# The y of a Hyena layer kept by thirds of the tokens in the storage of the projections' input, with the last two projections in a written order

## The chip, the cores and the metric

The kernel runs on one core of a Trainium2 chip. The metric is the device time of one execution in microseconds (us). The engines are TensorE (PE for matmuls, PEld for the weight loads that overlap them), VectorE (DVE), ScalarE (ACT), GpSimd (POOL) and SyncE (SP), which issues most of the DMAs. Each engine works its own instructions in the order in which they stand; semaphores order the engines against each other.

## The reference

Two layers over 1024 latent tokens (tiles 0 to 7 of 128) and 128 context tokens (tile 8), with width 1024. The part that matters here is the end of layer 0 (Hyena) and the start of layer 1 (attention):

```python
proj = h @ w_in                                   # 1024 -> 4096, 32 groups of 128 columns
u = short_conv(proj[..., :3 * HY_WIDTH], conv_w, conv_b)
gate = proj[..., 3 * HY_WIDTH:]
x0, x1, v = jnp.split(u, 3, axis=-1)
...                                               # y = long convolution of z = v * x1
y = (y + z * f_bias) * x0
out = (y * jax.nn.silu(gate)) @ w_out
x = x + g * out
h1 = rmsnorm(x, norm_w[1]) * (1.0 + scale) + shift
proj1 = h1 @ mla_w_in                             # the first projection of layer 1
```

## The kernel before, in words

Everything is float32. A product is made of three matmul passes: each operand is split into a high part (float32r, made on ACT or POOL by `hi`, L88 and L90) and the rest (`lo`, a subtraction on DVE or POOL, L96); high by high, high by rest and rest by high are summed in PSUM.

The input of layer 0, transposed (channels on the partitions), lies as three thirds of 384 tokens: `hT0` to `hT2` (high) and `lT0` to `lT2` (rest), each 128 x 8 x 384. A projection `in_proj` takes one of the 32 column groups of w_in: for each third 3 x 8 matmuls of 128x384. Its weights come in two halves (`wi_raw`, 256 KB each, issued on SP): ACT makes `wi_h` of a half and POOL `wi_l`. The convolved projections go through `conv_cb` (a copy into `u`) and `conv` (one instruction on ACT, two on DVE over all 1152 tokens).

The inverse transforms write y of each of the eight channel groups to HBM (`YD`) and later read it back (`y0` to `y7`, 576 KB each). Groups 6 and 7 are gated last, by `gate_group`: projection g, convolution, projection 24 + g, SiLU, product. For group 7 these are projections 7 and 31, the last two of all.

When projection 31 is done, the pool of the input (`hy`) is released, and `lhh0` to `lhh7`, `lhl0` to `lhl7` (one 128x1152 tile per channel group) take its place: eight `hi` on ACT and eight `lo` on DVE. `w_out` then multiplies tile by tile of the tokens, 24 matmuls of 128x512 per tile and half of the columns, adds to x, and `norm_mod` writes the input of layer 1 back over `lhh` and `lhl`, in pairs of tiles: a square and a root on ACT, a scaling `nm_x` on DVE, eight transposes per tile on PE, `nm_h` on ACT, high part on POOL, rest on DVE. The list `WT` groups the tiles: 0-3, 4-5, 6-7, 8. While the last tiles are normed, PE works on `mla_gate(0)` (L970), 144 matmuls of 128x384, of which 96 need only the first two thirds of the tokens.

The order of each engine's instructions is not that of the source: a scheduler sets it from a modelled timeline, with priorities (`urgent`) and lower bounds (`issue_after`). Within `manual_schedule` the named engines keep the written order; the others don't.

Of the kernel before, what the change touches and what calls it, by code (L numbers as in the profile page):

```python
# [17 lines left out]
P = 128  # L18
# [2 lines left out]
GATES = (0, None, None, 1, None, None, None, None)  # L21
NY = 6
YP, YG = (), ()
WT = ((0, 1, 2, 3), (4, 5), (6, 7), (8,))
XB = 4
PLAN = "g2 I0 a0 I1 g3 I2 a1 I3 g4 a2 g5 I4 a3 i5 i6 i7"
WRB = 3
# [48 lines left out]
class K:  # L76
# [107 lines left out]
    def norm_mod(self, xs, tiles, pool, ps, A, B, hT, lT):  # L184

        N = P * len(tiles)
        ys = [pool.tile([P, D], F32, name="nm_x", tag="nm_x", bufs=2) for _ in xs]
        self.norm(xs, ys, pool)
        c = 1 if tiles[0] == 8 else 0
        o = slice(P * tiles[0], P * tiles[0] + N)  # L190
        for k in range(8):
            pt = self.turn(ys, k, ps, "nm_ps", 3)
            h = pool.tile([P, 256], F32, name="nm_h", tag="nm_h", bufs=3)
            self.S.activation(h[:, :N], pt, AF.Identity, bias=B[:, k, c:c + 1], scale=A[:, k, c:c + 1])
            self.hi("pool", hT[k][:, o], h[:, :N])
            self.lo("dve", lT[k][:, o], h[:, :N], hT[k][:, o])
# [458 lines left out]
    def hyena(self):  # L655
# [141 lines left out]
        with self.urgent():  # L797
            for g in range(8):
                if g in late and g not in done:
                    self.gate_y(g, ys[g], q, yb)  # L800
        for g in range(8):
            if g not in GATES and g not in late:
                with tc.issue_after(last):
                    self.gate_group(g, q, ys[g])
        early.release()
        hy.release()
        lh = tc.alloc_tile_pool(name="lh", bufs=1, side="left", reuse_waits="tile")
        lhh, lhl = [], []
        for g in range(8):
            lhh.append(lh.tile([P, T], F32R, name=f"lhh{g}"))  # L810
            lhl.append(lh.tile([P, T], F32R, name=f"lhl{g}"))
            self.hi("pool" if g in HP else "act", lhh[g], ys[g])
            self.lo("pool" if g in YP else "dve", lhl[g], ys[g], lhh[g])
        yb.release()
        ips.release()
        A = self.small.tile([P, 8, 2], F32, name="ada_A1")
        self.ada_mod(1, m1, A, slice(0, 8))
        return lh, lhh, lhl, wp, wo, gd, (A, m1[:, 0:8, :])

    def w_out(self, px, wp, ps, lhh, lhl, wo, gd, A, B):  # L820

        nc, a = self.nc, self.a
        wo.append(self.load_w(a["w_out"][1], px, 512, "wo1", 1, raw_bufs=WRB, step=1))
        gb = self.load_gate(px, gd, "gb0")
        for tiles in WT:
            xs = [self.load_x(px, t, XB) for t in tiles]
            for h in range(2):
                o = slice(512 * h, 512 * h + 512)
                for x, t in zip(xs, tiles):
                    pt = ps.tile([P, 512], F32, name="wo_ps", tag="wo_ps", bufs=4)  # L830
                    self.mm3(pt, lhh, lhl, slice(P * t, P * t + P), *wo[h], 8)
                    tm = px.tile([P, 512], F32, name="wo_t", tag="wo_t", bufs=1)
                    self.tt(tm, pt, gb[:, 1 if t == 8 else 0, o], ALU.mult)
                    self.tt(x[:, o], x[:, o], tm, ALU.add, self.G)
            for x, t in zip(xs, tiles):
                nc.sync.dma_start(self.x1d[t], x)
            for i in range(0, len(tiles), 2):
                self.norm_mod(xs[i:i + 2], tiles[i:i + 2], px, ps, A, B, lhh, lhl)
# [74 lines left out]
    def mla_in(self, pool, wpool, ps, hT, lT, m):  # L913
        nc, a = self.nc, self.a
        qnh, qnl, ckh, ckl, kp = m["qnh"], m["qnl"], m["ckh"], m["ckl"], m["kp"]
        qkv = pool.tile([P, NT, 672], F32, name="qkv", bufs=1)
        for h in range(2):
            wh, wl = self.load_w(a["wm_a"][h], wpool, 336, "wm", 2, raw_bufs=2, step=1, tag_raw="wm_raw")
            for t in range(NT):
                pt = ps.tile([P, 512], F32, name="wo_ps", tag="wo_ps", bufs=4)  # L920
                self.mm3(pt[:, :336], hT, lT, slice(P * t, P * t + P), wh, wl, 8)
                self.S.copy(qkv[:, t, 336 * h:336 * h + 336], pt[:, :336])
        kvr = pool.tile([P, KVL], F32, name="kvr", bufs=1)
        nc.sync.dma_start(kvr, a["kv_norm"].partition_broadcast(P))
        rt = pool.tile([P, 2, 8, ROPE], F32, name="rope_k", bufs=1)
        nc.sync.dma_start(rt, a["rope_k"])
        rq, ck = [], []
        for t in range(NT):
            r = self.rstd(pool, qkv[:, t, 0:QL], QL, "q")
            self.V.tensor_scalar(qkv[:, t, 0:QL], qkv[:, t, 0:QL], r, None, ALU.mult)  # L930
            r = self.rstd(pool, qkv[:, t, QL:QL + KVL], KVL, "kv")
            kv = qkv[:, t, QL:QL + KVL]
            self.stt(kv, kv, r, kvr, ALU.mult)
        nc.sync.dma_start(a["s_ckv"], qkv[:, 8, QL:QL + KVL])
        nc.sync.dma_start(a["s_kpe"], qkv[:, 8, QL + KVL:672])
        for g in range(3):
# [24 lines left out]
    def mla_gate(self, h, pool, ps, hT, lT, GD, bufs):
        wh, wl = self.load_w(self.a["wm_g"][h], pool, 256, "wm", bufs, raw_bufs=2, step=1, tag_raw="wm_raw",
                             size=336 if h else 256)
        for o in range(0, T, 384):
            for i in range(2):
                w = slice(P * i, P * i + P)
                pt = ps.tile([P, 512], F32, name="wo_ps", tag="wo_ps", bufs=4)[:, :384]
                for k in range(8):
                    for s, (a, b) in enumerate(((wh, hT), (wl, hT), (wh, lT))):
                        self.PE.matmul(pt, a[:, k, w], b[k][:, o:o + 384], start=s == 0 and k == 0, stop=s == 2 and k == 7)  # L970
                g = pool.tile([P, 384], F32, name="gsil", bufs=GB)
                self.S.activation(g, pt, AF.Silu)
                (self.nc.sync if h else self.nc.scalar).dma_start(GD[2 * h + i][:, o:o + 384], g)
# [544 lines left out]
```

## Time and profile before

| | |
|---|---|
| time, median of 3 runs | 1785.12 us (1783.82 to 1785.66) |
| profiled execution | 1784.39 us |
| its span in the trace | 1782.2 us |
| busy: PE, PEld, DVE, ACT, POOL | 97%, 87%, 70%, 61%, 31% |
| chain that ended last | PE 75%, DVE 13%, DMA 4%, ACT 3%, issue 3% |
| mean granted TensorE clock | 0.997 |

The profiled execution is 2.2 us longer than its span, and 0.7 us below the median of the runs. PE is busy nearly throughout, so what a change in this stretch is worth is read from the few places at which PE has nothing to do, and from the clock that it is granted (1.00 is 2.4 GHz, 0.50 is 1.2 GHz). Times below are from the start of the span.

### The profile page before, as it was taken

The numbers are of one execution on the slowest core, as the hardware profiler recorded it, in microseconds if no ns is written. First come the engines' busy times: TensorE is split into PE (matmuls) and PEld (weight loads), VectorE is DVE, ScalarE is ACT, GpSimd is POOL, SyncE is SP. The second block draws the span as 40 slices with busy tenths as digits, with TensorE's granted clock in tenths as the row PEclk, the third lists the DMA queues.
The fourth block names the chain that finished last, engine by engine and source line by source line (L and its number), as shares of the span: only waits on it lengthen the run. The fifth ranks groups of instructions, "written<-read, shape, count | busy, mean of one in ns | idle before, by whom it ended". The sixth has DMA issues, their size and how long they took to land.

```text
span 1782.2 us, 29982 instructions
## 1 busy us (share of the span) xinstructions
PE 1728.2 (97%) x10704; PEld 1555.8 (87%) x10704; DVE 1245.5 (70%) x2515; ACT 1087.0 (61%) x2566; POOL 550.1 (31%) x771
## 2 busy tenths in 40 slices
PE   6999999999999999999999999999999999999998
PEld 4888889999999788888999889999999998999876
DVE  4658988999886895542242487878887888778464
ACT  7656557665654334324352587878887888788441
POOL 3335234343443101232000134433433343227300
PEclk9999999999999999999999999999999999999999
DMA  8233332111133856422213310100010010003351
GB/s 332 92 114 108 103 99 89 57 51 48 55 110 124 273 173 246 154 78 81 71 47 98 88 31 27 39 25 25 25 38 26 23 30 25 19 20 92 128 186 73
DMA packets 90488, 156.99 MB, mean 88 GB/s; under 512 B 11683, under 2 KB 57923, under 8 KB 88548
## 3 DMA queue, kind: packets, MB, share of 16 engines
q1 hardware_dynamic: 85744, 145.29, 24.8%
q0 software_dynamic: 2272, 6.38, 1.2%
q10 hardware_dynamic: 2324, 3.42, 0.6%
q8 instruction: 84, 1.38, 0.3%
q14 instruction: 64, 0.52, 0.1%
HBM read 113.92 MB, written 36.73 MB: 85 GB/s over the span
## 4 chain that ended last, share of the span: by engine, by line
PE 75%; DVE 13%; DMA 4%; ACT 3%; issue 3%; POOL 2%; SPq 0%; DVEq 0%; ACTq 0%; POOLq 0%
PE wo_ps L627 14%; PE wo_ps L1309 12%; PE ip_ps L426 10%; PE av_ps L1193 9%; PE nm_ps L1181 7%; PE wo_ps L970 5%; PE wo_ps L1005 5%; PE iv_ps L556 3%; PE df_ps L375 2%; DMA wi_raw<-w_in 2%; DVE pr_o L99 2%; DVE cv L102 1%; PE nm_ps L1037 1%; DVE O L102 1%; POOL wi_l L96 1%
## 5 line engine op out<-in xcount | busy, mean ns | idle before, releaser
L1309 PE MATMUL wo_ps<-kT,qT 128*128 128x512 f32 (+1 forms) x1152 | 278.7, 372 | 4.9 <-ACT prob L1316 4.4
L1316 ACT ACTIVATE prob<-wo_ps,mx 128x512 f32<-128x512 f32 (+1 forms) x384 | 234.1, 618 | 13.0 <-DVE mx L1314 11.1
L88 ACT ACTIVATE pt_h<-nm_ps 128x512 fp32r<-128x512 f32 x324 | 192.9, 599 | 74.0 <-PE nm_ps L1181 67.1
L1312 DVE TENSOR_REDUCE mx<-wo_ps 128x1 f32<-128x512 f32 (+1 forms) x384 | 213.0, 596 | 22.7 <-PE wo_ps L1309 22.1
L1309 PEld LDWEIGHTS wo_ps<-kT,qT 128*128 128x128 f32 x1152 | 187.4, 189 | 39.4 <-ACT prob L1316 14.4
L96 DVE TENSOR_TENSOR pt_l<-nm_ps,pt_h 128x512 fp32r<-128x512 f32 x324 | 210.5, 683 | 14.6 <-ACT pt_h L88 10.4
L96 POOL TENSOR_TENSOR wi_l<-wi_raw,wi_h 128x512 fp32r<-128x512 f32 x64 | 121.6, 1900 | 243.7 <-ACT wi_h L88 238.2
L1181 PE MATMUL nm_ps<-ident,prob 128*128 128x128 f32 x1280 | 191.4, 272 | 0.0
L426 PE MATMUL ip_ps<-hT,wi_h 128*128 128x384 f32 x720 | 153.0, 343 | 5.9 <-ACT wi_h L88 5.9
L1181 PEld LDWEIGHTS nm_ps<-ident,prob 128*128 128x128 f32 x1280 | 149.9, 140 | 8.5
L426 PE MATMUL ip_ps<-lT,wi_h 128*128 128x384 f32 x720 | 154.0, 342 | 0.0
L426 PE MATMUL ip_ps<-hT,wi_l 128*128 128x384 f32 x720 | 150.1, 342 | 0.0
L426 PEld LDWEIGHTS ip_ps<-hT,wi_h 128*128 128x128 f32 x720 | 126.1, 189 | 14.6 <-ACT wi_h L88 6.8
L1193 PE MATMUL av_ps<-pt_h,Vt 128*128 128x256 f32 x640 | 137.8, 297 | 0.0
L1193 PE MATMUL av_ps<-pt_l,Vt 128*128 128x256 f32 x640 | 135.0, 292 | 0.1
L426 PEld LDWEIGHTS ip_ps<-lT,wi_h 128*128 128x128 f32 x720 | 126.9, 189 | 5.2 <-issue 2.5
L426 PEld LDWEIGHTS ip_ps<-hT,wi_l 128*128 128x128 f32 x720 | 126.6, 189 | 5.5 <-issue 2.1
L99 POOL TENSOR_TENSOR pr<-ev 128x256 f32<-128x256 f32 x72 | 77.0, 1075 | 130.0 <-ACT ev L383 75.4
L1193 PEld LDWEIGHTS av_ps<-pt_l,Vt 128*128 128x128 f32 x640 | 97.6, 188 | 8.2 <-DVE pt_l L96 2.1
L1193 PEld LDWEIGHTS av_ps<-pt_h,Vt 128*128 128x128 f32 x640 | 97.9, 189 | 0.2
L102 DVE SCALAR_TENSOR_TENSOR cv<-u,cols,cv 128x1153 f32<-128x1153 f32 x48 | 75.7, 1578 | 11.8 <-ACT cv L451 11.7
L1200 POOL COPY rr<-sm 128x128 f32<-128x128 f32 x64 | 18.4, 288 | 202.4 <-DVE sm L1199 201.8
(355 smaller groups left out, 4083.1 us busy)
## 6 DMA issues: line engine op xcount, KB each, us to landing
wi_raw<-w_in SPq DMA_DIRECT2D x64, 256.0 KB, 3.0
ada_w<-ada_w SPq DMA_DIRECT2D x12, 1024.0 KB, 7.4
ada_w<-ada_w SPq DMA_DIRECT2D x24, 512.0 KB, 3.9
x_in<-xs SPq DMA_DIRECT2D x16, 512.0 KB, 5.2
PS<-pr_o SPq DMA_DIRECT2D x64, 128.0 KB, 1.9
pi_raw<-PS SPq DMA_DIRECT2D x32, 256.0 KB, 4.0
YD<-yv SPq DMA_DIRECT2D x8, 576.0 KB, 3.5
y<-YD SPq DMA_DIRECT2D x8, 576.0 KB, 9.1
```

The source lines that it names most:

```text
L88: self.S.activation(out, src, AF.Copy)
L96: e.tensor_tensor(out, src, hi.bitcast(F32), ALU.subtract)
L99: (eng or self.V).tensor_tensor(out, x, y, op)
L102: self.V.scalar_tensor_tensor(out, x, s, y, op0, op1)
L426: mm = self.PE.matmul(pt, w[:, k, :], x[c][:, k, :], start=s == 0 and k == 0, stop=s == 2 and k == 7)
L627: self.PE.matmul(pt, x[k][:, sl], w[:, k, :], start=s == 0 and k == 0, stop=s == 2 and k == kt - 1)
L970: self.PE.matmul(pt, a[:, k, w], b[k][:, o:o + 384], start=s == 0 and k == 0, stop=s == 2 and k == 7)
L1181: self.PE.transpose(pt[:, P * i:P * i + P], u["p"][i % 2][n // 2][:, P * (2 * (n % 2) + i // 2):P * (2 * (n % 2) + i // 2) + P], self.ident)
L1193: self.PE.matmul(u["po"][:, :256], m["V"][:, 2 * n + e, j, :], u[n][1 + s][:, 256 * e:256 * e + 256], start=n == first and e + s == 0, sto ...
L1309: self.PE.matmul(pt[:, :n], x[:, j, P * i:P * i + P], y[:, j, o:o + n], start=s == 0, stop=s == 2)
L1312: self.V.tensor_reduce(mx[:, b:b + 1], c["s", i, b][:, :n], AX.X, ALU.max)
L1316: self.S.activation(c["p"][i][b], c["s", i, b][:, :n], AF.Exp, bias=c["mx"][i][:, 3:4], accum_out=c["sm"][:, i, b:b + 1])
```

## The change

y is no longer split as a whole into sixteen tiles after the last projection. It is split by thirds of the tokens, and each third takes the tile of the input third that it replaces (`hT0`, `lT0` and so on, by their names), as soon as both last projections have read that third. A new `gate_last` does group 7: projections 7 and 31 run for the first two thirds, then for the last one; the order of ACT and DVE there is written out; the product with y and its split are made per third. `w_out` takes its tiles by three, three, two and one, and `norm_mod`, still in pairs, so norms tiles 2 and 5 alone. What reads the thirds later (`tokens`) is changed to match.

```diff
-WT = ((0, 1, 2, 3), (4, 5), (6, 7), (8,))
+WT = ((0, 1, 2), (3, 4, 5), (6, 7), (8,))
...
@@ norm_mod
-        o = slice(P * tiles[0], P * tiles[0] + N)
+        third, o = tiles[0] // 3, P * (tiles[0] % 3)
+        o = slice(o, o + N)
+        hT, lT = ([x[third][:, k] for k in range(8)] for x in (hT, lT))
...
@@ hyena
-        for g in range(8):
-            if g not in GATES and g not in late:
-                with tc.issue_after(last):
-                    self.gate_group(g, q, ys[g])
+        with tc.issue_after(last):
+            self.gate_group(6, q, ys[6])
+            lhh, lhl = self.gate_last(7, q, hy, ys)
         early.release()
-        hy.release()
-        lh = tc.alloc_tile_pool(name="lh", bufs=1, side="left", reuse_waits="tile")
-        lhh, lhl = [], []
-        for g in range(8):
-            lhh.append(lh.tile([P, T], F32R, name=f"lhh{g}"))
-            lhl.append(lh.tile([P, T], F32R, name=f"lhl{g}"))
-            self.hi("pool" if g in HP else "act", lhh[g], ys[g])
-            self.lo("pool" if g in YP else "dve", lhl[g], ys[g], lhh[g])
...
+    def gate_last(self, g, q, hy, ys):
...
+        def weights(i):
+            k = slice(4 * i, 4 * i + 4)
+            raw = pool.tile([P, 4, P], F32, name="wi_raw", bufs=1)
+            self.nc.sync.dma_start(raw, self.a["w_in"][24 + g][:, k])
+            self.hi("act", hs[0][:, k], raw)
+            self.lo("pool", hs[1][:, k], raw, hs[0][:, k])
+
+        def project(w, c):
+            pt = q["ips"].tile([P, 384], F32, name="ip_ps", tag="ip_ps", bufs=3)
+            for s, (a, x) in enumerate(((w[0], self.hT), (w[0], self.lT), (w[1], self.hT))):
+                for k in range(8):
+                    self.PE.matmul(pt, a[:, k, :], x[c][:, k, :], start=s == 0 and k == 0, stop=s == 2 and k == 7)
+            return pt
...
+        def product(c):
+            for o, o_, n in parts(c):
+                self.tt(gt[:, o:o + n], gt[:, o:o + n], x0[:, o:o + n], ALU.mult)
+                self.tt(y[:, o_:o_ + n], y[:, o_:o_ + n], gt[:, o:o + n], ALU.mult)
+
+        def split(c, gs):
+            if lhh[c] is None:
+                lhh[c], lhl[c] = (hy.tile([P, 8, 384], F32R, name=f"{x}T{c}") for x in "hl")
+            for i in gs:
+                x = ys[i][:, 384 * c:384 * c + 384]
+                self.hi("act", lhh[c][:, i], x)
+                self.lo("dve", lhl[c][:, i], x, lhh[c][:, i])
+
+        with self.tc.manual_schedule(engines={E.Activation, E.DVE}):
+            weights(0)
+            self.conv_cb(project(w0, 0), 0, q)
+            weights(1)
+            self.conv_cb(project(w0, 1), 384, q)
+            silu(project(hs, 0), 0)
+            split(0, range(7))
+            silu(project(hs, 1), 1)
+            self.conv_cb(project(w0, 2), 768, q)
+            x0 = self.conv(g, q)
+            split(1, range(7))
+            for c in range(2):
+                product(c)
+                split(c, (7,))
+            silu(project(hs, 2), 2)
+            product(2)
+            split(2, range(8))
```

Upstream of projection 7 no engine's order is changed; from there to the end of the last norm they are.

On PE, the last two projections before the change: `wi_h_7109` and `wi_l_7110` are the weights of projection 7, `wi_h_7202` and `wi_l_7203` those of projection 31; the number after `ip_ps` tells the third's accumulator, and x4 are the matmuls of one half of the weights.

```order
L426 MATMUL ip_ps_7213<-hT1_123,wi_l_7110 128x384 x8
L426 MATMUL ip_ps_7239<-hT2_125,wi_l_7110 128x384 x8
L426 MATMUL ip_ps_7239<-lT2_126,wi_h_7109 128x384 x8
L426 MATMUL ip_ps_7239<-hT2_125,wi_h_7109 128x384 x8
L426 MATMUL ip_ps_7271<-hT0_121,wi_h_7202 128x384 x4
L426 MATMUL ip_ps_7297<-hT1_123,wi_h_7202 128x384 x4
L426 MATMUL ip_ps_7323<-hT2_125,wi_l_7203 128x384 x4
L426 MATMUL ip_ps_7271<-hT0_121,wi_h_7202 128x384 x4
```

And with the change (projection 7 as before, projection 31 with `wi_h_7177` and `wi_l_7178`):

```order
L835 MATMUL ip_ps_7216<-hT1_123,wi_l_7110 128x384 x8
L835 MATMUL ip_ps_7242<-hT0_121,wi_h_7177 128x384 x4
L835 MATMUL ip_ps_7284<-hT1_123,wi_h_7177 128x384 x4
L835 MATMUL ip_ps_7242<-hT0_121,wi_h_7177 128x384 x4
L835 MATMUL ip_ps_7242<-lT0_122,wi_h_7177 128x384 x8
L835 MATMUL ip_ps_7242<-hT0_121,wi_l_7178 128x384 x4
L835 MATMUL ip_ps_7284<-hT1_123,wi_h_7177 128x384 x4
L835 MATMUL ip_ps_7284<-lT1_124,wi_h_7177 128x384 x2
L835 MATMUL ip_ps_7242<-hT0_121,wi_l_7178 128x384 x4
L835 MATMUL ip_ps_7284<-lT1_124,wi_h_7177 128x384 x6
L835 MATMUL ip_ps_7284<-hT1_123,wi_l_7178 128x384 x8
L835 MATMUL ip_ps_7310<-hT2_125,wi_h_7109 128x384 x8
```

Before, all of projection 7 and the first half of projection 31 for three thirds stand ahead of the first matmul that needs the second half of the weights. Now 28 matmuls fewer stand there: the last third of projection 7 (24) is behind it, and so are four of the last third of 31.

On SP, the loads around that second half (`wi_raw`), with `y5` to `y7` the read-back of y and `w_raw` weights of w_out. Before:

```order
L796 DMA y5_6942<-YD5_109 128x1152
L410 DMA wi_raw_7208<-w_in 128x512
L796 DMA y6_6943<-YD6_110 128x1152
L619 DMA w_raw_6975<-w_out 128x512
L796 DMA y7_6944<-YD7_111 128x1152
L619 DMA w_raw_7419<-w_out 128x512
L619 DMA w_raw_7423<-w_out 128x512
L619 DMA w_raw_7427<-w_out 128x512
```

With the change:

```order
L799 DMA y5_6942<-YD5_109 128x1152
L799 DMA y6_6943<-YD6_110 128x1152
L799 DMA y7_6944<-YD7_111 128x1152
L622 DMA w_raw_6975<-w_out 128x512
L827 DMA wi_raw_7212<-w_in 128x512
L622 DMA w_raw_7444<-w_out 128x512
L622 DMA w_raw_7448<-w_out 128x512
L622 DMA w_raw_7452<-w_out 128x512
```

The second half of the weights of projection 31 is now issued behind y6, y7 and a piece of w_out instead of ahead of them.

On PE, near the end of the norms: `nm_ps` x4 are the last transposes of tiles 6 and 7, x5 the first of tile 8, and the `wo_ps` rows between are the gate projection of layer 1. Before, 32 matmuls stand between the two, of which the first rows are:

```order
L181 MATMUL nm_ps<-ident,nm_x 128x128 x4
L970 MATMUL wo_ps<-lhh_7379,wm_l 128x384
L970 MATMUL wo_ps<-lhl_7380,wm_h 128x384
L970 MATMUL wo_ps<-lhh_7383,wm_h 128x384
L970 MATMUL wo_ps<-lhh_7383,wm_l 128x384
L970 MATMUL wo_ps<-lhl_7384,wm_h 128x384
```

With the change there are 6:

```order
L182 MATMUL nm_ps<-ident,nm_x 128x128 x4
L1035 MATMUL wo_ps<-hT_7341,wm_h 128x384
L1035 MATMUL wo_ps<-hT_7341,wm_l 128x384
L1035 MATMUL wo_ps<-lT_7342,wm_h 128x384
L1035 MATMUL wo_ps<-hT_7341,wm_h 128x384
L1035 MATMUL wo_ps<-hT_7341,wm_l 128x384
L1035 MATMUL wo_ps<-lT_7342,wm_h 128x384
L182 MATMUL nm_ps<-ident,nm_x 128x128 x5
```

The 26 others stand ahead of the x4 now; ACT's and DVE's instructions between the two are the same as before.

## Rows read from the trace of the kernel before

**Rows 1.** The page, busy time of PE with its share of the span and count.

```profile
PE 1728.2 (97%) x10704; PEld 1555.8 (87%) x10704; DVE 1245.5 (70%) x2515; ACT 1087.0 (61%) x2566; POOL 550.1 (31%) x771
```

**Rows 2.** Stretches: length, busy PE PEld DVE ACT POOL, granted clock, DMA share, GB/s.

```profile
685.80:690.70 4.90, 4.90 (x28) 4.45 (x26) 1.39 (x2) 2.70 (x5) 0.00 (x0) 1.00 1.02 402
690.70:692.80 2.10, 0.00 (x1) 0.00 (x0) 1.34 (x2) 0.97 (x2) 0.00 (x0) 1.00 1.04 406
692.80:694.25 1.45, 1.44 (x8) 1.44 (x9) 1.45 (x3) 0.01 (x1) 1.42 (x1) 1.00 1.04 406
694.25:697.65 3.40, 3.40 (x13) 3.40 (x12) 3.40 (x3) 0.63 (x1) 1.04 (x1) 0.52 1.06 410
697.65:705.10 7.45, 7.42 (x43) 7.10 (x41) 0.86 (x2) 0.99 (x2) 0.00 (x0) 0.99 0.15 60
705.10:706.76 1.66, 0.00 (x0) 0.00 (x0) 1.23 (x2) 1.65 (x4) 0.00 (x0) 1.00 0.00 0
706.76:755.80 49.04, 49.03 (x211) 39.52 (x212) 28.75 (x38) 18.98 (x29) 11.19 (x8) 1.00 0.41 138
```

**Rows 3.** The chain that ended last, in order of time: start, length, what.

```profile
692.81 12.28 PE ip_ps L426 x60
```

**Rows 4.** Timeline of SP's issues (start, length, line, out<-in, count).

```profile
680.86 1.75 SPq L796 DMA_DIRECT2D y<-YD  x2
683.79 0.33 SPq L410 DMA_DIRECT2D wi_raw<-w_in  x1
...
685.89 0.33 SPq L619 DMA_DIRECT2D w_raw<-w_out  x1
686.50 0.32 SPq L796 DMA_DIRECT2D y<-YD  x1
```

**Rows 5.** Timeline of DVE and ACT: first users of what SP loaded.

```profile
691.46 1.36 DVE L99 TENSOR_TENSOR y<-y,xg 128x1152 f32<-128x1152 f32 x1 [1.51 <-DMA y<-YD]
692.13 0.63 ACT L88 ACTIVATE wi_h<-wi_raw 128x512 fp32r<-128x512 f32 x1 [1.08 <-DMA wi_raw<-w_in]
694.25 0.63 ACT L88 ACTIVATE wo_h<-w_raw 128x512 fp32r<-128x512 f32 x1 [1.49 <-DMA w_raw<-w_out]
```

**Rows 6.** The page, DMA issues: count, KB each, median us to landing.

```profile
wi_raw<-w_in SPq DMA_DIRECT2D x64, 256.0 KB, 3.0
...
y<-YD SPq DMA_DIRECT2D x8, 576.0 KB, 9.1
```

**Rows 7.** Timelines of ACT and DVE: convolution, and instructions on a third's 384 columns.

```profile
647.44 0.56 DVE L99 TENSOR_TENSOR bf<-bf 128x384 f32<-128x384 f32 x1
...
689.14 0.36 ACT L443 COPY u<-ip_ps 128x256 f32<-128x256 f32 x1
...
689.69 1.35 ACT L451 ACTIVATE cv<-u,cols 128x1153 f32<-128x1153 f32 x1
...
696.50 1.41 DVE L102 SCALAR_TENSOR_TENSOR cv<-u,cols,cv 128x1153 f32<-128x1153 f32 x1
...
701.64 0.49 ACT L508 ACTIVATE cv<-ip_ps 128x384 f32<-128x384 f32 x1 [1.24 <-PE ip_ps L426]
```

**Rows 8.** Timelines of ACT and DVE: the split of y, then second-half weights of w_out.

```profile
705.55 8.54 ACT L88 ACTIVATE lhh<-y 128x1152 fp32r<-128x1152 f32 x8
...
718.36 1.89 DVE L96 TENSOR_TENSOR wo_l<-w_raw,wo_h 128x512 fp32r<-128x512 f32 x3
```

**Rows 9.** The chain near the end of the norms (as Rows 3).

```profile
825.53 0.44 PE nm_ps L181 x4
825.97 5.56 PE wo_ps L970 x32
```

**Rows 10.** Timelines of ACT, DVE and PE in the same stretch.

```profile
826.25 1.05 ACT L171 ACTIVATE nm_x<-x_in 128x1024 f32<-128x1024 f32 x1
...
828.24 1.28 ACT L172 ACT_TABLE_LOAD   x1
...
830.12 0.75 DVE L176 TENSOR_SCALAR nm_x<-x_in,nm_r 128x1024 f32<-128x1024 f32 x1
...
831.35 0.49 PE L181 MATMUL nm_ps<-ident,nm_x 128*128 128x128 f32 x3
...
832.44 0.68 PE L181 MATMUL nm_ps<-ident,nm_x 128*128 128x128 f32 x2 [0.60 <-ACT nm_h L194]
```

More of the change, by code (lines that the diff above doesn't have):

```diff
@@ L817, in hyena, with parts, silu @@
         self.ada_mod(1, m1, A, slice(0, 8))
-        return lh, lhh, lhl, wp, wo, gd, (A, m1[:, 0:8, :])
+        return hy, lhh, lhl, wp, wo, gd, (A, m1[:, 0:8, :])
+    def gate_last(self, g, q, hy, ys):
+        assert q["order"][q["n"]] == g and q["order"][q["n"] + 1] == 24 + g
+        pool, u, y = q["early"], q["u"], ys[g]
+        w0, w1 = q["w"], [[], []]
+        hs = [pool.tile([P, 8, P], F32R, name="wi_" + x, bufs=2) for x in "hl"]
+        gt = pool.tile([P, 1153], F32, name="cv", bufs=3)
+        lhh, lhl = [None] * 3, [None] * 3
+        def weights(i):
[10 more added lines that the diff above has]
+            return pt
+        def parts(c):
+            return ((384 * c, 384 * c, 384),) if c < 2 else ((768, 768, 256), (1025, 1024, P))
+        def silu(pt, c):
+            d = 0
+            for o, _, n in parts(c):
+                self.S.activation(gt[:, o:o + n], pt[:, d:d + n], AF.Silu)
+                d += n
+        def product(c):
[9 more added lines that the diff above has]
+                self.lo("dve", lhl[c][:, i], x, lhh[c][:, i])
+        E = mybir.EngineType
+        with self.tc.manual_schedule(engines={E.Activation, E.DVE}):
[15 more added lines that the diff above has]
+            split(2, range(8))
+        return lhh, lhl
@@ L820, in w_out, with tokens @@
+    def tokens(self, x, t):
+        return [x[t // 3][:, k, P * (t % 3):P * (t % 3) + P] for k in range(8)]
     def w_out(self, px, wp, ps, lhh, lhl, wo, gd, A, B):
@@ L830, in w_out @@
                     pt = ps.tile([P, 512], F32, name="wo_ps", tag="wo_ps", bufs=4)
-                    self.mm3(pt, lhh, lhl, slice(P * t, P * t + P), *wo[h], 8)
+                    self.mm3(pt, self.tokens(lhh, t), self.tokens(lhl, t), slice(0, P), *wo[h], 8)
                     tm = px.tile([P, 512], F32, name="wo_t", tag="wo_t", bufs=1)
@@ L920, in mla_in @@
                 pt = ps.tile([P, 512], F32, name="wo_ps", tag="wo_ps", bufs=4)
-                self.mm3(pt[:, :336], hT, lT, slice(P * t, P * t + P), wh, wl, 8)
+                self.mm3(pt[:, :336], self.tokens(hT, t), self.tokens(lT, t), slice(0, P), wh, wl, 8)
                 self.S.copy(qkv[:, t, 336 * h:336 * h + 336], pt[:, :336])
@@ L969, in mla_gate @@
                     for s, (a, b) in enumerate(((wh, hT), (wl, hT), (wh, lT))):
-                        self.PE.matmul(pt, a[:, k, w], b[k][:, o:o + 384], start=s == 0 and k == 0, stop=s == 2 and k == 7)
+                        self.PE.matmul(pt, a[:, k, w], b[o // 384][:, k], start=s == 0 and k == 0, stop=s == 2 and k == 7)
                 g = pool.tile([P, 384], F32, name="gsil", bufs=GB)
```

## The prediction, made before the changed kernel ran

> **What bounds the kernel now.** The page first: PE is busy 97% of the span [rows 1], so time can come or go only where PE stands still or is granted half its clock. The windows over the last projections and the start of w_out show three such places [rows 2]. PE stops at 690.70 for 2.10 us. After its restart the granted clock is 0.52 from 694.25 to 697.65. From 705.10 to 706.76 PE stops again, for 1.66 us. From there w_out runs without a stop: 49.04 us for 211 matmuls, 0.2325 us each.
>
> What ends the first stop is read on ACT: the high part of the second half of the weights of projection 31 begins at 692.13 and waited for the DMA of `wi_raw` [rows 5]; PE restarts at 692.81 [rows 3]. The second stop is the split of y: the first of eight high parts begins at 705.55, and one takes 8.54 / 8 = 1.07 us [rows 8], so w_out begins at 706.76. In the norms there is one more place to look at: the chain of waits passes through 32 gate matmuls between the last transposes of tiles 6 and 7 and the first of tile 8 [rows 9], under which ACT and DVE norm tile 8.
>
> **Step 1: the second half of the weights of projection 31.** PE now has 28 matmuls fewer ahead of the first one that needs this half. The window from 685.80 to 690.70 holds exactly 28, at 4.90 / 28 = 0.175 us each, at full clock [rows 2]. So PE stops at 685.80 instead of 690.70.
>
> At the same time the load is moved back on SP: y5, y6, y7, a piece of w_out, `wi_raw`, where it stood second. Its place is the fifth, at which y7 was issued, at 686.50 [rows 4]: already after PE has stopped. When does it land? Before, y5 had landed at 691.46, `wi_raw` (256 KB) at 692.13 and y6 with w_out's piece (576 + 256 = 832 KB) at 694.25, in the order of their issue [rows 5, 6]. That is 2.12 us for 832 KB, 2.55 ns per KB, with the DMA engines full (share 1.04 to 1.06, 406 to 410 GB/s [rows 2]). Now y6, y7, the piece of w_out and `wi_raw`, 576 + 576 + 256 + 256 = 1664 KB, follow on y5: 1664 x 2.55 ns = 4.24 us, so 695.70. (The median of 9.1 us from issue to landing of a y [rows 6], put on 686.50, gives 695.6.) ACT's high part adds what it added before, 692.81 - 692.13 = 0.68: PE restarts at 696.4. The wait is 10.6 us instead of 2.1, +8.5. Bounds: if the load overtook everything and took its own median of 3.0 us [rows 6], it would land at 689.5 and PE restart at 690.2, 6.2 us earlier; if y7 is held up, SP's fifth issue comes behind 320 KB more than before, 0.8 us later. I take 10.6, since every landing in these rows was in the order of issue.
>
> The Trainium skill ("DMA: Bandwidth & Descriptors", section "Queues, rings and completion order") says that completion is not first in, first out per issuing engine. By that rule the small load could land ahead of y6 and y7, which is the rival at 690.2. The trace shows no such overtaking here, though it has the same mix: 256 KB behind 576 KB.
>
> **Clock.** Before, 60 matmuls after the restart took 12.28 us [rows 3]; at 0.1745 each they are 10.47, so the clock cost 1.8. It rose at 697.65, 4.84 us after the restart. After a wait five times as long I expect half clock from the restart itself: 4.84 / 2 = 2.4. Bounds: 0 if it doesn't fall; the same 4.84 at half clock twice, 4.8. I take 2.4, +0.6.
>
> That longer waits don't keep the clock up is also what the Trainium skill says ("TensorE: Matmul & The Clock Gate", section "What's actually happening"): the throttled state is the default, and activity releases it. By the rule alone the loss is 2.4, by the row repeated 1.8.
>
> Of the 144 matmuls of the two projections 56 stand ahead of the stop. The other 88 take 88 x 0.175 = 15.4: from 696.4 with the clock's 2.4 w_out's first matmul starts at 714.2, against 706.76.
>
> **Step 2: y by thirds.** The 1.66 us of waiting for the split go: groups 0 to 6 of the first third are split under PE's work on the projections. In their place stands group 7, which w_out needs at its 22nd matmul (three per group). Its chain starts when the last third of projection 7 ends, 24 matmuls ahead of w_out: copies to `u` 0.55 (from 689.14 to 689.69), convolution 1.35 on ACT and 2 x 1.41 on DVE, then by the written order seven rests of the second third ahead of the product, 7 x 0.56, the product 2 x 0.56, and the high part 0.49 [rows 7]: 10.25 us. PE's cover is 24 x 0.175 + 21 x 0.2325 = 9.1. So a new stall of 1.2 us, against 1.66 gone: -0.5. Bounds: 0, if DVE gets ahead with the split; 3.6, if copies and convolution queue behind the SiLUs as long as 2.4 us.
>
> So far: +8.5 + 0.6 - 0.5 = +8.6.
>
> Of the rest of the split nothing is on the path. DVE has, from the end of the convolution at 710.0 + 4.7 = 714.7, 3.9 (second third), two times product, high and rest (2 x 2.2), product, high and eight rests of the last third (6.1): until 729.1. Only then come the three rests of w_out's second column half, 1.89 us [rows 8]: ready at 731.0, 10.7 later than before. PE needs them after three tiles now, 715.4 + 72 x 0.2325 = 732.1. About 1 us is left. If that cover is gone, each us of lateness is a us of stall.
>
> **Step 3: the norm of tile 8.** ACT's and DVE's instructions between the transposes of tiles 6 and 7 and those of tile 8 are the same, but PE has 6 matmuls there instead of 32; 26 moved ahead. From 825.53 to the end of the scaling at 830.12 + 0.75 = 830.87 the chain takes 5.3 us (square 1.05, table load 1.28, scaling 0.75 and small ones [rows 10]); the 32 matmuls took 5.56 [rows 9] and hid it with 831.35 - 830.87 = 0.5 to spare. Now the chain starts 26 x 0.1745 = 4.5 later relative to PE's work, so PE waits 4.5 - 0.5 = 4.0. Some 0.4 of the 0.60 us that PE waited for `nm_h` behind it [rows 10] comes back, since the copies are then done: +3.6. Bounds: 0, if ACT starts the square of tile 8 ahead of these copies; 4.5 + 1.8 = 6.3, if the clock falls again as at 694.25. I take 3.6, as ACT's order sets the start.
>
> The norms of tiles 2 and 5 alone stand beside two tiles of w_out or more, and cost nothing while w_out lasts.
>
> **Sum.** 8.6 + 3.6 = +12.2 on the profiled execution's 1784.4: 1796.6. The median of the runs lies 0.7 above it: 1797.
>
> **Rivals.**
> *Tail hidden.* The 26 matmuls moved cost nothing, because the chain of tile 8 runs off x_in, which is loaded early. For it: the square reads x_in and not the copies. Against it: ACT is in order and PE's transposes release its copies first. 1797.3 - 3.6 = 1793.7.
> *Overtaking.* `wi_raw` lands 3.0 us after its issue: 6.2 less, 1791.
> *Faster.* One mechanism decides the entry: whether PE waits for the second half. If the half is there when PE arrives, the 2.1 us, the clock's 1.8 and the 1.66 go and 1.2 comes: -4.4, with a hidden tail 1784.4 - 4.4 + 0.7 = 1780.7. The change is slower as soon as the wait with its clock loss exceeds 4.4 us. For it: the 1.66 us of the split go in any case, and y is the larger load. Against it: PE arrives at 685.80 and the issue is at 686.50.
> *More than forecast.* The rests of w_out's second half late, or the clock down again in the tail: 1801 to 1806.
> *The thirds don't do what the change says*: the split is still waited for, since DVE is behind with the written order. The stall of step 2 then is 3.6 rather than 1.2: 1799.7, inside the forecast's range.
>
> **How the numbers follow.** About 0.2%, 3.6 us, is what a measurement can tell from no change here. Forecast 0.58 (its own range 1793 to 1801, from the bounds of the clock, the stall and the tail), tail hidden 0.15, overtaking 0.08, more 0.14, faster 0.05. The range that leaves out the faster case and the far ends: 1790 to 1803. Faster is the one case, 0.05; within 0.2% would take overtaking and a hidden tail together, 0.03; slower 0.92.
>
> **What would show it.** Step 1: PE idle from 685.8 to about 696, ended by `wi_h`, whose DMA lands near 695.7 behind y7 and not ahead; granted clock near 0.5 for some 5 us after. A restart before 691 is the overtaking; no stop at all the faster case. Step 2: w_out begins at 714 without a wait for a high part at its first matmul, and stops about 1 us at its 22nd, ended by the third's group 7. Step 3: PE idle about 4 us ahead of the transposes of tile 8, ended by `nm_x`. A stop at the second column half, ended by a rest of w_out, is the cover of 1 us gone. The prediction is wrong if the time is below 1790, above all if SP's issues of y6 and y7 wait and `wi_raw` goes past them.

## The result and the profile after

The changed kernel takes 1800.43 us (median of 5 runs, 1799.59 to 1801.46) against 1785.66 us (1783.82 to 1786.40): ratio 1.0088, 95% interval 1.0075 to 1.0100. Between the medians it is slower by 14.8 us, where +12.2 was forecast (1797 us, range 1790 to 1803). The profiled execution is one of 1801.24 us with a span of 1799.4 us.

PE's busy line first; the line of the kernel before is in [rows 1]. PE has the same 10704 matmuls, but is busy for 5.7 us longer (1733.9 against 1728.2) in a span that is 17.2 us longer. So the loss stands mostly in stops between the matmuls, and for about a third in the clock at which they ran:

```profile
PE 1733.9 (96%) x10704; PEld 1560.4 (87%) x10704; DVE 1249.5 (69%) x2544; ACT 1091.3 (61%) x2591; POOL 549.9 (31%) x779
```

PE's waits from 670 to 900 us (engine, line, what it waited for: us in total, times, longest). Before, the same view had 2.1 us for `wi_h`, 1.7 for `lhh`, 0.6 for `nm_h` and 2.9 for `wm_h`:

```profile
PE ip_ps L835 <- ACT wi_h L89: 11.2, 1, 11.2
PE nm_ps L182 <- DVE nm_x L177: 4.7, 2, 4.0
PE wo_ps L630 <- ACT wm_h L89: 2.2, 2, 1.6
PE wo_ps L630 <- ACT hT L89: 0.8, 1, 0.8
```

The same stretches as windows (columns as in [rows 2]; the column before the last two is the granted clock): the stop for the weights, the half clock behind it, the rest of the projections, w_out up to its 22nd matmul, the stop there, then a stop at the transposes of tile 2 (754.08), the one at tile 8 (841.19) and the half clock behind that.

```profile
685.04:696.24 11.20, 0.00 (x0) 0.00 (x0) 5.46 (x7) 2.57 (x5) 0.00 (x0) 0.62 1.04 406
696.24:702.21 5.97, 5.97 (x20) 5.97 (x21) 0.01 (x1) 0.32 (x1) 1.27 (x1) 0.56 0.35 143
702.21:714.00 11.79, 11.79 (x69) 11.79 (x69) 5.33 (x9) 7.69 (x18) 0.00 (x0) 1.00 0.00 0
714.00:719.06 5.06, 5.06 (x22) 3.76 (x21) 5.03 (x10) 0.86 (x3) 0.00 (x0) 1.00 0.00 0
719.06:719.83 0.77, 0.01 (x2) 0.01 (x1) 0.18 (x2) 0.52 (x1) 0.00 (x0) 1.00 0.00 0
...
754.08:754.81 0.73, 0.00 (x0) 0.00 (x0) 0.73 (x2) 0.00 (x0) 0.00 (x0) 1.00 0.00 0
841.19:845.19 4.00, 0.00 (x0) 0.03 (x1) 1.62 (x4) 2.78 (x6) 0.40 (x1) 0.96 0.14 49
845.19:851.50 6.31, 6.18 (x20) 5.53 (x21) 1.74 (x6) 2.52 (x6) 1.89 (x6) 0.50 0.00 0
```

**The entry.** SP issues the last three y without `wi_raw` between them, then the piece of w_out, then `wi_raw` (answers to [rows 4]):

```profile
680.71 4.83 SPq L799 DMA_DIRECT2D y<-YD  x4
685.76 0.33 SPq L622 DMA_DIRECT2D w_raw<-w_out  x1
686.43 0.33 SPq L827 DMA_DIRECT2D wi_raw<-w_in  x1
```

The chain of waits has the transfer itself (start, length) and what follows:

```profile
686.43 9.11 DMA wi_raw<-w_in
695.56 0.64 ACT wi_h L89
```

So it landed at 695.54, behind the piece of w_out, whose high part began at 694.89 (answers to [rows 5]). PE restarted at 696.24.

**The end of the norms.** PE's rows around the last transposes of tiles 6 and 7 (x4) and the first of tile 8 (answers to [rows 9, 10]):

```profile
839.54 0.60 PE L182 MATMUL nm_ps<-ident,nm_x 128*128 128x128 f32 x4
...
840.85 0.34 PE L1035 MATMUL wo_ps<-lT,wm_h 128*128 128x384 f32 x1
845.19 0.87 PE L182 MATMUL nm_ps<-ident,nm_x 128*128 128x128 f32 x3 [4.01 <-DVE nm_x L177]
```

ACT's square and table load for tile 8 come, as before, behind the copy of the last transposes:

```profile
839.96 0.56 ACT L197 ACTIVATE nm_h<-nm_ps,ada_m,ada_A 128x256 f32<-128x256 f32 x1 [2.46 <-PE nm_ps L182]
840.42 1.05 ACT L172 ACTIVATE nm_x<-x_in 128x1024 f32<-128x1024 f32 x1
...
842.41 1.28 ACT L173 ACT_TABLE_LOAD   x1
```

From the first transposes of tile 8 to the first matmul of the next weights (`wm_a`) it took 843.40 - 831.35 = 12.05 us before, and takes 859.48 - 845.19 = 14.29 us now: 2.24 us more, the cost of the half clock less the 0.6 us that PE waited there before.

### The profile page after: what moved, and what is told of

Its sections match the earlier page's. It is cut to its first block, busy times and chain, and to the rows that moved or that the text cites. A ratio compares the mean times of both kernels' runs of the same rounds, so it can differ in the third digit from the quotient of the medians.

```text
span 1799.4 us, 30046 instructions
## 1 busy us (share of the span) xinstructions
PE 1733.9 (96%) x10704; PEld 1560.4 (87%) x10704; DVE 1249.5 (69%) x2544; ACT 1091.3 (61%) x2591; POOL 549.9 (31%) x779
## 4 chain that ended last, share of the span: by engine, by line
PE 71%; DVE 15%; DMA 6%; ACT 3%; issue 3%; POOL 2%; SPq 0%; DVEq 0%; ACTq 0%; POOLq 0%
PE wo_ps L1374 11%; PE wo_ps L630 11%; PE ip_ps L429 9%; PE av_ps L1258 8%; PE nm_ps L1246 7%; PE wo_ps L1035 5%; PE wo_ps L1070 5%; PE iv_ps L559 3%; PE df_ps L378 2%; DMA wi_raw<-w_in 2%; DVE cv L103 2%; DVE pr_o L100 2%; PE nm_ps L1102 1%; DVE ab_lo L97 1%; DVE O L103 1%
## 5 line engine op out<-in xcount | busy, mean ns | idle before, releaser
L97 POOL TENSOR_TENSOR wi_l<-wi_raw,wi_h 128x512 fp32r<-128x512 f32 x64 | 117.9, 1843 | 245.3 <-ACT wi_h L89 239.8
L429 PE MATMUL ip_ps<-hT,wi_h 128*128 128x384 f32 x672 | 143.3, 343 | 3.7 <-ACT wi_h L89 3.7
L429 PE MATMUL ip_ps<-lT,wi_h 128*128 128x384 f32 x672 | 143.9, 342 | 0.0
L429 PE MATMUL ip_ps<-hT,wi_l 128*128 128x384 f32 x672 | 140.1, 341 | 0.0
L429 PEld LDWEIGHTS ip_ps<-hT,wi_h 128*128 128x128 f32 x672 | 117.2, 188 | 12.1 <-ACT wi_h L89 4.3
L429 PEld LDWEIGHTS ip_ps<-lT,wi_h 128*128 128x128 f32 x672 | 118.1, 188 | 5.2 <-issue 2.5
L429 PEld LDWEIGHTS ip_ps<-hT,wi_l 128*128 128x128 f32 x672 | 117.7, 188 | 5.3 <-issue 1.7
```

What stands on the lines that cost most here:

```text
L97: e.tensor_tensor(out, src, hi.bitcast(F32), ALU.subtract)
L429: mm = self.PE.matmul(pt, w[:, k, :], x[c][:, k, :], start=s == 0 and k == 0, stop=s == 2 and k == 7)
```

## The experiments

All ratios are to runs of the kernel before on the same chip, whose median was 1783.5 us in the first four, 1784.6 in the next four and 1784.8 in the last four. A ratio isn't exactly that of the two medians, and differences of 2 us between experiments are within their intervals; what such a difference consists of is read from the traces.

**1. The load ahead again.** `load` of the second half with the old priority:

```diff
-            self.nc.sync.dma_start(raw, self.a["w_in"][24 + g][:, k])
+            with self.urgent():
+                self.nc.sync.dma_start(raw, self.a["w_in"][24 + g][:, k])
```

> The changed kernel, with the second half of the weights of projection 31 loaded ahead of y6 again (the DMA alone has the old priority); PE's order stays. Theory (entry = late place on SP plus 28 matmuls fewer as cover, added): the load lands near 692.1 instead of 695.6, PE restarts near 692.8 instead of 696.2, the idle time is 7.7 us instead of 11.2, the rest unchanged: 1800.4 - 3.4 = 1797.0. Rival (the place in the queue doesn't matter, because the DMA engines are full and share): no change, 1800.

Measured: 1798.16 us, ratio 1.0077 (1.0062 to 1.0092). PE's restart:

```profile
694.68 1.65 PE L836 MATMUL ip_ps<-hT,wi_h 128*128 128x384 f32 x4 [8.59 <-ACT wi_h L89]
```

The stop is 2.6 us shorter (3.4 expected): the place on SP is a part of the wait, and not the larger one. The time alone doesn't show it, since the interval overlaps that of the changed kernel (1.0075 to 1.0100).

**2. The order on PE back.**

```diff
+            self.conv_cb(project(w0, 2), 768, q)
+            x0 = self.conv(g, q)
             silu(project(hs, 0), 0)
             split(0, range(7))
             silu(project(hs, 1), 1)
-            self.conv_cb(project(w0, 2), 768, q)
-            x0 = self.conv(g, q)
```

> The changed kernel, with the last third of projection 7 and its convolution ahead of projection 31 again; the load stays behind y6 and y7. Theory: 24 matmuls (4.2 us) cover the wait, PE stops near 689.2, restarts at 696.2 as before, idle 7.0 us instead of 11.2; w_out begins 4.2 us earlier, and the stall of 0.8 us at its 22nd matmul goes, because the convolution is done during the wait: 1800.4 - 5.0 = 1795.4. Rival (the order on PE only moves the wait): w_out begins as late as now, 1800.

Measured: 1794.60 us, 1.0058 (1.0043 to 1.0073). The restart, with the load still fifth:

```profile
698.46 1.65 PE L835 MATMUL ip_ps<-hT,wi_h 128*128 128x384 f32 x4 [7.48 <-ACT wi_h L89]
```

The stop is 3.7 us shorter, and the wait for the third's high part is no longer in the list of waits: the time is as expected within 1 us.

**3. Both.**

> Both edits together; y is still split by thirds. Theory: the two add: restart near 692.8, idle 3.6 us, w_out near 706.4 without a stall, so the entry costs nothing against the kernel before, and what is left is the end of the norms: 1800.4 - 8.4 = 1792. Rival (the split by thirds itself holds w_out up): w_out waits for a high part at its start or at the 22nd matmul, and the time is 1794 or more.

Measured: 1792.16 us, 1.0043 (1.0026 to 1.0059). The stop, and w_out's first matmul without one:

```profile
694.52 1.65 PE L836 MATMUL ip_ps<-hT,wi_h 128*128 128x384 f32 x4 [4.47 <-ACT wi_h L89]
708.66 0.39 PE L630 MATMUL wo_ps<-wo_h,hT 128*128 128x512 f32 x1
```

Against the 11.2 us of the changed kernel that is 6.7 us less, where the two parts alone gave 2.6 + 3.7 = 6.3: they add. But they aren't all of it. The expectation had a stop of 3.6 us and w_out at 706.4; the stop is 4.47, 2.4 us longer than before the change, and w_out begins at 708.66 instead of 706.76. PE arrives 0.65 us earlier than before (690.05 against 690.70), because four of the 28 matmuls aren't put back, and the y ahead of the load is used 1.7 us later (691.46 before [rows 5]):

```profile
693.18 1.36 DVE L100 TENSOR_TENSOR y<-y,xg 128x1152 f32<-128x1152 f32 x1 [1.54 <-DMA y<-YD]
```

Why that y is late isn't shown. 8.6 us over the kernel before remain between the medians, 1.9 of them at the start of w_out.

**4. The grouping alone.** The kernel before with one line:

```diff
-WT = ((0, 1, 2, 3), (4, 5), (6, 7), (8,))
+WT = ((0, 1, 2), (3, 4, 5), (6, 7), (8,))
```

> The kernel before, with nothing but the grouping of the tiles by three, three, two and one; y is split as a whole, the projections are untouched. Theory (the end of the norms is lost by the grouping alone, through the order that the scheduler then gives PE): w_out begins at 706.8 as before, and PE waits 4 us or more ahead of the transposes of tile 8, with half clock behind: 1785.7 + 6 to 9 = 1793. Rival (the tail comes from the late entry or from the tiles of the thirds): no change, 1786.

Measured: 1791.90 us, 1.0045 (1.0030 to 1.0060), +8.4 us. The two waits of its entry for `wi_h` and `lhh` are those of before. The stop ahead of tile 8 is new, and so is one of 1.7 us in projection 31 (689.26 to 690.98), for which the profile names no cause ("issue"):

```profile
PE nm_ps L181 <- DVE nm_x L176: 4.9, 1, 4.9
PE ip_ps L426 <- ACT wi_h L88: 2.1, 1, 2.1
...
PE ip_ps L426 <- issue: 1.7, 1, 1.7
PE wo_ps L627 <- ACT lhh L88: 1.7, 1, 1.7
```

Its windows of the stop and of what follows it:

```profile
834.28:839.19 4.91, 0.00 (x0) 0.03 (x1) 2.51 (x6) 3.55 (x6) 1.64 (x4) 0.87 0.07 26
839.19:845.00 5.81, 5.68 (x19) 5.03 (x20) 1.74 (x6) 2.53 (x6) 1.89 (x6) 0.52 0.00 0
```

So the stop at the end of the norms needs neither a late entry nor tiles by thirds; it comes with the grouping. Not all of the 8.4 us is this stop: at w_out's 49th matmul this trace is already 1.8 us behind (719.90 against 718.07): 1.2 at w_out's first matmul, with the unnamed stop ahead of it, and 0.6 in the 48 that follow. From the first transposes of tile 8 to the first matmul of `wm_a` it takes 13.88 us, 1.83 more than before, so stop and half clock cost 4.9 + 1.8 = 6.7 us.

That it works through the order that PE is given, the traces show as a series. The length of the stop follows the number of gate matmuls between the last transposes of tiles 6 and 7 and the first of tile 8: 32 and no stop (before), 10 and 2.94 us (experiments 1 and 3), 6 and 4.01 us (the changed kernel and experiment 2), none and 4.92 and 4.83 us (experiments 4 and 7). In experiment 3:

```profile
836.27 0.87 PE L182 MATMUL nm_ps<-ident,nm_x 128*128 128x128 f32 x3 [2.94 <-DVE nm_x L177]
```

**5. A third buffer for the normed tile.** With two buffers, the norm of tile 8 can't begin before one that tile 6 or 7 holds is free:

```diff
-        ys = [pool.tile([P, D], F32, name="nm_x", tag="nm_x", bufs=2) for _ in xs]
+        ys = [pool.tile([P, D], F32, name="nm_x", tag="nm_x", bufs=3) for _ in xs]
```

> The changed kernel, with three buffers instead of two for the normed tile (nm_x), so that tile 8 can be normed before tiles 6 and 7 are transposed to the end. Theory (the end of the norms is lost because the chain of tile 8 has 26 gate matmuls less as cover, and half clock follows on the stop): the stop of 4.0 us ahead of the transposes of tile 8 and the 2.2 us of half clock go, the entry stays: 1800.4 - 6 = 1794.4. Rival (tile 8 is normed late whatever the buffers, since ACT and DVE work in order): the stop stays, 1800.

Measured: 1796.50 us, 1.0070 (1.0057 to 1.0084). No wait for `nm_x` is left, but a new one has come:

```profile
PE ip_ps L835 <- ACT wi_h L89: 11.8, 1, 11.8
PE wo_ps L630 <- ACT wo_h L89: 2.9, 1, 2.9
```

The stop went as the theory says. What the estimate missed: w_out's second column half is now late, and half clock follows (0.60 in the next 4.2 us). Its first three loads begin at 725.07 instead of 687.82; SP's own list of waits has them behind a product with y on DVE:

```profile
SPq L622 <- DVE y L100: 35.9, 1, 35.9
```

**6. The same buffer in the kernel before.**

> The kernel before with three buffers for the normed tile, nothing else: what this edit is worth without the change. Theory: before, 32 gate matmuls covered the chain, so only the 0.6 us of waiting in the transposes of tile 8 can go: 0 to -1 us, 1784.5 against 1785 (the same). Rival (the buffer is worth as much here as in the changed kernel): -6, 1779.

Measured: 1781.75 us, 0.9988 (0.9980 to 0.9997): 2.9 us between the medians, 2.1 by the ratio, more than the 0.6 us of the wait and less than the rival. From the start of w_out to the first matmul of `wm_a` it takes 135.5 us instead of 136.6. The rest is not settled: this trace is already 1.2 us ahead where PE stops for `wi_h` (689.51 against 690.70), upstream of what was edited.

**7. The weights in buffers of their own, ahead of y.** PE's order stays as changed.

```diff
-            raw = pool.tile([P, 4, P], F32, name="wi_raw", bufs=1)
-            self.nc.sync.dma_start(raw, self.a["w_in"][24 + g][:, k])
+            raw = yb.tile([P, 4, P], F32, name=f"wi_raw{i}", bufs=1)
+            with self.urgent():
+                self.nc.sync.dma_start(raw, self.a["w_in"][24 + g][:, k])
```

> The changed kernel, with the weights of projection 31 loaded ahead of all of y, each half into a buffer of its own; PE's order stays as changed (two thirds first). Theory (with the load in time the mechanism of the faster case holds at the entry): PE doesn't stop at 685, keeps its clock, and w_out begins near 700 instead of 714; its 22nd matmul then waits for the third's group 7, up to 5 us, because y and the chain on ACT and DVE don't come earlier by as much: 1800.4 - 13.7 + 4 = 1791, with the end of the norms as in the changed kernel. Rival (the transfers of y, all of which are needed, set the entry): PE stops as long as now at another place, 1798 or more.

Measured: 1786.05 us, 1.0009 (1.0000 to 1.0018). The projections from where PE had stopped, and w_out's first 22 matmuls, as windows:

```profile
685.00:700.20 15.20, 15.20 (x90) 15.20 (x88) 9.26 (x14) 8.85 (x19) 0.00 (x0) 1.00 0.69 271
700.20:705.26 5.06, 5.06 (x22) 3.76 (x21) 5.03 (x10) 1.19 (x3) 0.00 (x0) 1.00 0.00 0
```

No stop, no half clock; w_out begins at 700.20, 6.6 us earlier than before, and its 49th matmul comes 5.2 us earlier. Its longest waits:

```profile
PE nm_ps L182 <- DVE nm_x L177: 5.1, 2, 4.8
PE wo_ps L630 <- ACT wm_h L89: 2.0, 2, 1.6
PE wo_ps L630 <- ACT hT L89: 1.1, 1, 1.1
```

The 22nd matmul waits 1.1 us, not up to 5 as expected. So two thirds first is no loss at the entry once the weights are there; the time is that of before within 0.2%, since the end of the norms, with its stop of 4.8 us, takes it back.

**8. The edits of 2, 5 and 7 together.**

> The changed kernel with three edits: the weights of projection 31 ahead of y in buffers of their own, projection 7 whole ahead of projection 31 again, three buffers for the normed tile; y stays split by thirds in the input's storage. Theory: nothing is left of the three costs, and the 2.1 us, the clock's 1.8 and the 1.66 us of the kernel before are gone as well: faster than before by 4 to 6 us, 1779. Rival (the loads of y, late by the 256 KB that go ahead, or the split by thirds hold w_out up): a stop of 3 us or more at w_out's first 22 matmuls, 1783 or more, no better than before.

Measured: 1780.56 us, 0.9981 (0.9972 to 0.9990). Faster than before, by 3.4 us by the ratio. Where the rest went:

```profile
PE wo_ps L630 <- ACT wm_h L89: 2.2, 2, 1.5
PE wo_ps L630 <- ACT wo_h L89: 2.1, 1, 2.1
```

w_out starts 5.7 us earlier than before, and from its 97th matmul it is only 1.9 us ahead.

**9. The third buffer allocated first in its pool**, so that what is loaded early keeps its place.

> As the kernel with all three edits, but the three nm_x buffers are allocated first in their pool, so that the staging of w_out's second half doesn't move onto the memory of the convolutions (in the run before, its first three loads began at 709.2 instead of 685.2, and PE stopped 2.1 us with half clock behind, 4.0 in all). Theory: the loads begin at 685 again and the stop shrinks to the 0.5 us of the run with its own load buffers: 1780.6 - 3.5 = 1777. Rival (the later pieces of w_out decide, which are behind 2.5 MB of gate rows and x on SP in any case): the stop stays, 1780.5.

Measured: 1780.16 us, 0.9975 (0.9966 to 0.9984). Only the first of the three loads is early again; the other two are issued at 710.10, and the wait is 1.8 instead of 2.1 us:

```profile
685.30 0.33 SPq L622 DMA_DIRECT2D w_raw<-w_out  x1
710.10 0.81 SPq L622 DMA_DIRECT2D w_raw<-w_out  x2
```

The time is the rival's, but the theory wasn't put to the test: its condition, three loads at 685, was met for one of them. Whether the first three pieces decide is not shown.

**10. The gate rows and x issued behind the fifth piece.**

> As e9, with the gate rows and x of the first tiles issued behind the fifth piece of w_out's second half. Theory (the pieces were late because they are behind 2.5 MB): no stop in w_out, 1776.5 to 1777. Rival (now the additions wait for x and hold the four accumulators): a stop at the 97th matmul of w_out, 1779 or more.

Measured: 1782.07 us, 0.9986 (0.9977 to 0.9995). The waits for w_out's weights are broken into several and are not shorter in sum, so the theory didn't hold; the rival named another cause, the additions, and these rows don't show it:

```profile
PE wo_ps L630 <- ACT wo_h L89: 2.0, 2, 1.2
...
PE wo_ps L630 <- DVE wo_l L97: 1.0, 2, 0.7
```

SP here issues two loads of the gate weights (`wm_raw`) ahead of the fourth piece, and the second and third piece are as late as in experiment 9; whether either is the cause wasn't tried.

**11. The kernel before with the edits of 5 and 7, without thirds.**

> The kernel before with the weights of projection 31 in buffers of their own ahead of y and three nm_x buffers; y split as a whole, no thirds: what the edits are worth without the change. Theory: the 2.1 us of waiting for the weights and the clock's 1.8 go beside the 2 us of the third buffer, the 1.66 us of waiting for the split stay: 1784.6 - 2.1 - 3.9 = 1778.6, and the thirds are worth at most the 1.7 that remain. Rival (the gain of the kernel with all three edits came from the thirds): 1782 as with the buffer alone.

Measured: 1778.37 us, 0.9972 (0.9961 to 0.9982). Of its waits only the split of y is left at the entry:

```profile
PE wo_ps L627 <- ACT wm_h L88: 2.0, 3, 1.5
PE wo_ps L627 <- ACT lhh L88: 1.7, 1, 1.7
```

So the thirds aren't needed for the gain: their version, experiment 9, has 0.9975.

**12. As 9, with w_out by four, two, two and one** (tiles 2 and 3 normed alone).

```diff
-WT = ((0, 1, 2), (3, 4, 5), (6, 7), (8,))
+WT = ((0, 1, 2, 3), (4, 5), (6, 7), (8,))
-            for i in range(0, len(tiles), 2):
-                self.norm_mod(xs[i:i + 2], tiles[i:i + 2], px, ps, A, B, lhh, lhl)
+            for i, n in ((0, 2), (2, 1), (3, 1)) if len(tiles) == 4 else ((0, 2),):
+                self.norm_mod(xs[i:i + n], tiles[i:i + n], px, ps, A, B, lhh, lhl)
```

> As e9, with the tiles of w_out by four, two, two and one as in the kernel before, tiles 2 and 3 normed alone; y stays by thirds. Theory (the stop in w_out's second column half comes because three tiles cover 72 matmuls, 16.7 us, of the loads of that half where four covered 96, 22.3 us): the stop of 1.8 us and the half clock behind it, 3.6 in all, go, 1780.2 - 3.6 = 1776.6, a little below the 1778.4 of e11. Rival (the loads are late by as much whatever the grouping, or the two norms alone cost what the stop did): 1780.

Measured: 1778.07 us (5 runs, 1775.49 to 1780.60), 0.9960 (0.9946 to 0.9973). The stop in w_out is nearly gone:

```profile
PE wo_ps L630 <- ACT wm_h L89: 2.3, 2, 1.5
PE wo_ps L630 <- ACT wo_h L89: 0.4, 1, 0.4
PE wo_ps L630 <- DVE wo_l L97: 0.2, 1, 0.2
```

So the cover of w_out's second half was the grouping's: 96 matmuls instead of 72. This version beats both kernels; by time it can't be told apart from experiment 11, nor from experiment 9, and what the grouping gave is read from the waits.

## Why the prediction was right, and where it was short

- **Step 1, the wait: right.** PE stopped at 685.04 (forecast 685.80), `wi_raw` was issued at 686.43 (686.50), landed at 695.54 (695.7), PE restarted at 696.24 (696.4). The stop is 11.2 us and not 10.6 because PE arrives 0.76 us earlier; the two traces differ by 0.7 us already at 680, ahead of the change. Nothing overtook, neither here nor in experiment 2, where the load stood at the same place and was used right behind the piece of w_out. The rule of the Trainium skill ("DMA: Bandwidth & Descriptors", section "Queues, rings and completion order") that completion is not first in, first out doesn't show in these landings. The prediction read more into it than it says: the section's example is a later transfer on one DMA engine against an earlier one on sixteen, and it has each engine's completion count land after all earlier writes of that engine. So for loads that are spread over the same 128 partitions, as all of these are, it doesn't speak for the rival. Experiments 1 to 3 show that the wait has the two parts named, cover taken away (3.7 us) and load put back (2.6 us), and that they add; with both edits 2.4 us of the additional 9.1 remain, of which four matmuls are 0.65.
- **Clock at the entry: right.** From 696.24 to 714.00 88 matmuls took 17.76 us; at 0.175 they are 15.4. The loss is 2.4, as taken. The granted clock was 0.56 over the 5.97 us from the restart on. (The 2.4 was the row's 4.84 us halved, and not a size that the rule quoted beside it gives.)
- **Step 2: the size a little high.** The stall at the 22nd matmul is 0.77 (forecast 1.2), because seven rests of a third took 3.36 and not 7 x 0.56 = 3.92 us. w_out's first matmul came at 714.00 (714.2). Its 49th came 8.3 us later than before: the +8.6 of the entry was right.
- **The cover of about 1 us for w_out's second half held**: three rests of it were made from 727.57 to 729.46 (forecast 729.1 to 731.0), and PE didn't stop. That it was thin shows in experiments 7 to 10, which come to w_out 13 us earlier than the changed kernel and stop there, for 0.5 us in experiment 7 and about 2 us in 8 and 9. (In experiment 5 it was the loads that came later.)
- **Step 3, mis-sized.** The term was "+3.6". The stop itself was the 4.0 us worked out, 4.01 by the row, and the 0.6 behind it went whole. But half clock followed for 6.31 us, which stood in the text only as the upper bound and as a case with a chance of 0.14: 2.24 us net. So the step cost 4.0 + 2.24 = 6.2, the bound of 6.3. Experiment 4 shows the same alone, with 4.91 us of stop and 0.52 granted for 5.8 us behind it. The row at the entry [rows 2], where a stop of 2.1 us already had half clock behind it, spoke for taking it here; in the fourteen traces all 12 stops of 2.9 us or more have it. How much it costs is less certain: in experiment 2 the clock behind the same stop of 4.01 us was half for a shorter time:

```profile
840.69:847.00 6.31, 5.96 (x26) 5.37 (x27) 1.74 (x6) 2.70 (x7) 1.88 (x6) 0.73 0.00 0
```

- **"The norms of tiles 2 and 5 alone ... cost nothing": wrong by 0.7.** PE waits 0.73 us at 754.08 for tile 2's `nm_x`; its chain was not set against the end of the first three tiles.
- **The sum.** 8.3 at the entry, 0.7 at tile 2 and 6.2 at tile 8 are 15.2, against 14.8 between the medians; 12.2 was forecast. The two traces are further apart than these terms: 16.1 us at the first matmul of `wm_a`, so 0.8 us between w_out's 49th matmul and the first transposes of tile 8 has no term. At the first stop of layer 1's attention they restart at 1016.05 and 1031.84, 15.8 apart. Behind this stop, of 2.5 us in both, the trace before has full clock and the one after half clock, which puts them 17.1 apart at 1036.06; 1.0 us comes back by 1044.54, and the last 1.1 us up to the end of the span have no part in the change that I can name. The windows of 4 us behind the stop, before and after:

```profile
1016.05:1020.05 4.00, 4.00 (x18) 3.02 (x19) 1.18 (x3) 3.04 (x10) 0.00 (x0) 1.00 0.00 0
1031.84:1035.84 4.00, 4.00 (x13) 3.33 (x14) 1.22 (x3) 2.90 (x9) 0.00 (x0) 0.59 0.00 0
```

- **The rivals.** *Tail hidden*: no, 4.0 us of stop. *Overtaking*: no. *Faster*: its mechanism was real and its condition not met. Experiment 7 meets it, the weights there before PE: w_out begins 6.6 us earlier than before and is 5.2 us ahead at its 49th matmul, where 4.4 was priced. *Thirds held up by DVE*: no. *More than forecast*: half of it, the clock in the tail; the rests of w_out's second half weren't late.

## What to carry to other kernels

When a written order takes matmuls away from in front of a load, work out both sides: how much cover goes, and at which place of the queue the load is now issued; the two add. The stop of 4 us was priced right only with the clock behind it. So look for all stops of about that length which the traces already have, and take what follows them there as a range and not as one value: a single row can mislead, since the trace before has stops of 2.33 and 2.49 us with full clock behind them beside the one of 2.1 us with half. A regrouping that looks like bookkeeping (three tiles instead of four) changes what covers the next weights and the next norm; here it cost 6.9 us where the entry cost 8.3.

## What the runs showed of the hardware

Stops of PE and the granted clock behind them, all from these traces: behind 1.66 us (before, 705.10) w_out ran at 1.00, and behind 0.77 us (719.06) at 1.00. Behind 2.1 us 0.52 was granted for 3.4 us, beginning 1.4 us after the restart; behind 2.14 us (experiment 8) 0.60 over the next 4.2 us; behind 4.0 us 0.50 for 6.3 us from the restart on; behind 11.2 us 0.56 for 6.0 us. So 4.0 us cost as much clock as 11.2 us did, which I hadn't expected, though in experiment 2 the same 4.01 us cost less (0.73 over 6.31 us).

Counted over all fourteen traces of this case, half clock follows none of 25 stops of 1.5 to 1.72 us (one more has a longer stop right behind it), both of those of 1.75 and 1.78 us, 24 of the 32 of 2.1 to 2.5 us, and all 12 of 2.9 us or more. At 2.1 to 2.5 us the same place of the program goes either way: the stop in layer 1's attention has full clock behind it in the kernel before and half clock in the changed one, and the one near 76 us has full clock in both (1.00 over 4 us) and half clock in nine of the twelve experiments (0.63 in experiment 1). Two traces can differ by an us or more through this alone, as by the 1.3 us at 1036.06 above, wherever the change is. The Trainium skill ("TensorE: Matmul & The Clock Gate", section "What's actually happening") calls the throttled state the default that activity releases; the half clock behind every stop of 2.9 us or more agrees with that.

An edit of 4 KB per partition (experiment 5) moved loads by 37 us (687.82 to 725.07), with no instruction of theirs changed: SP held them until a product with y on DVE was done, so the larger pool seems to have laid their buffers onto memory that comes free only then; no run shows the addresses. Experiment 9 put the buffer first in the pool, and one of the three loads went back to 685.
